# The overflow rows of the next pair are gathered under the branch of the overflow's second product

## The chip, the cores and the metric

The kernel runs on one core of a Trainium2 chip. The metric is the time on the device in microseconds; times of several runs are given as their median with the lowest and highest. A profile is one more execution under the hardware profiler, with a time of its own.

## What is computed

One layer of a diffusion backbone with 256 latent and 256 context tokens of width 1024: four parallel token mixers (attention, neighbourhood attention, Fourier mixing, convolution), merged and projected, and then a mixture of 16 experts, each token going to two of them. The change concerns the experts alone:

```python
out = jnp.zeros_like(t)
for e in range(N_EXPERTS):
    a, b = jnp.split(t @ w_gu[e], 2, axis=-1)
    out = out + gate[:, e:e + 1] * ((jax.nn.silu(a) * b) @ w_down[e])
```

`gate[:, e]` is zero for a token that isn't routed to expert `e`, so the kernel computes only the rows of the tokens routed there. How many these are is known only when the program runs: 32 per expert on average (256 tokens, two of 16 experts each).

## The kernel before, in words

The token mixers and the routing come first; the experts start some 430 us into the span. Experts are taken in 8 pairs (`for pair in range(NPAIR)`, line 1154). Each expert has slots for its rows in blocks of 32. The first block of both experts of a pair is always computed. The second (rows 33 to 64) stands under `tc.If(both)` (lines 1167 and 1202), the third and fourth (rows 65 to 128, 64 rows at once, "the overflow") under two nested branches: the outer asks whether either expert of the pair overflows (line 1126, a bit of the register `fpair`), the inner whether this expert does (line 1128, a bit of `fmore`). Rows beyond 128 have a part of their own behind all pairs (line 1212).

The branches run on TensorE, VectorE and ScalarE, each with its own copy of the flags. On the way past a branch an engine's sequencer computes the bit and compares it (two instructions); where the body is skipped it goes to a false block, which waits until the engine's own earlier work is done and raises its semaphore by what the body would have added, and then joins the rest.

The overflow of one expert has three parts:

- `more_gather(e)` (line 960): a one-hot matrix of the rows from the routing keys (VectorE, `ohv`), 8 matmuls that gather the rows (`gav`), two copies to SBUF (`rw`, one on ScalarE and one on VectorE), the gate values (`gsv`), 8 transposes (`gtv`) and 8 modulations in turn on VectorE and ScalarE (`hgv`).
- `more_up(e, hg)` (line 988): the first product, 16 matmuls with w_gu (`guv`, in the records two for each), then silu and the product with the other half (`siv`).
- `more_down(e, gsl, si)` (line 999): the transposed hidden rows (`htv`, `hTv`), their places (`otv`, `oTv`), the second product with w_down (`yv`), the gate (`ysv`), the split in two parts (`yhv`, `ylv`), and the scatter by matmuls onto the tokens (`scv`), which VectorE adds to `xs`.

A pair runs in this order on TensorE: the first product of the first blocks (`gu`), under `both` that of the second blocks, the overflow's first product, the gates (`gs`), the scatter of the pair before (`sce`, from its `Y`), the hidden rows transposed (`ht`), the places of the rows (`ote`, from the keys that POOL copies into `kr`), in pairs 1, 3 and 5 the gather of the next two pairs (`gag`), the overflow rows of the next pair, the second product (`y`, begun with a product by zeros that clears a bank), under `both` that of the second blocks, the overflow's second product with its scatter. Then `gated` (line 892) takes `y` times gate on VectorE and splits it, and the next pair begins. For pair 0 the overflow rows are gathered directly ahead of its first product, under a branch of their own. The framework's scheduler moves some matmuls of a product behind the branches that follow it in the text: in the trace the last 12 records of `y` and `gu` stand behind them.

The weights come from HBM by SP's queue, 1 MB per transfer, 12 transfers per pair, into 18 slots in all; a transfer waits until TensorE has read what was in its slot. All DMAs of the change's surroundings are these; the change itself holds none.

Of the kernel before, what the change touches and what calls it, by code (L numbers as in the profile page):

```python
# [54 lines left out]
def mixer_moe(ctx: ExitStack, tc: tile.TileContext, A, out, dbg=None):  # L55
# [18 lines left out]
    def pt(tag, name):  # L74
        return banks["pool"].tile([P, 512], F32, tag=tag, bufs=banks["n"][tag], name=name)
# [4 lines left out]
    def sc_t(name):  # L80
        return pt("sc", name)

    def tr_t(name):
        return pt("tr", name)
# [651 lines left out]
    def scr_t(*shape):  # L736
        n = int(np.prod(shape))
        t = scratch[:, n_scratch[0] : n_scratch[0] + n]
        n_scratch[0] += n
        axes = "abc"[: len(shape)]  # L740
        return t.rearrange(f"p ({' '.join(axes)}) -> p {' '.join(axes)}", **dict(zip(axes[1:], shape[1:])))
# [17 lines left out]
    two = scr_t(N8, 2, 4)  # L759
# [51 lines left out]
    def mm(*a, **k):  # L811
        tc.keep_in_program_order(PE.matmul(*a, **k))  # L812

    def tr(*a):
        tc.keep_in_program_order(PE.transpose(*a))
# [29 lines left out]
    def modulated2(dst, src, k):  # L845
        if k % 2:
            SC.activation(dst, src, AF.Identity, scale=a2[:, k : k + 1], bias=sh2[:, k : k + 1])
        else:
            V.tensor_scalar(dst, src, a2[:, k : k + 1], sh2[:, k : k + 1], op0=ALU.mult, op1=ALU.add)
# [110 lines left out]
    def more_gather(e):  # L960

        oh = onehot(f"v{e}", lambda t: key[:, t, e : e + 1], CAP, "ohv", 1)
        rows = ep.tile([P, 2, 512], F32, name=f"rw{e}", tag="ys", bufs=1)
        for h in range(2):
            g = sc_t(f"gav{e}{h}")
            i = 0
            for t in range(NT):
                for src in (xh, xl):
                    mm(g[:CAP, :], oh[t], src[:, t, 512 * h : 512 * h + 512], start=(i == 0), stop=(i == 2 * NT - 1))
                    i += 1  # L970
            (V.tensor_copy if h else SC.copy)(rows[:CAP, h, :], g[:CAP, :])
        tp = tr_t(f"gsv{e}")
        for p in range(2):
            for t in range(NT):
                mm(tp[64 * p : 64 * p + 64, 0:2], oh[t].bitcast(F32), gate[:, t, e : e + 1].to_broadcast([P, 2]),
                   start=(t == 0), stop=(t == NT - 1))
        gsl = ep.tile([P, 1], F32, name=f"gslv{e}", tag="gslv", bufs=4)
        V.tensor_copy(gsl, tp[:, 0:1])
        hg = ep.tile([P, NK, CAP], F32, name=f"hgv{e}", tag="hgv", bufs=2)
        tp = tr_t(f"gtv{e}")  # L980
        for k in range(NK):
            d = tp[:, CAP * k : CAP * (k + 1)]
            tr(d, rows[:CAP, k // 4, P * (k % 4) : P * (k % 4 + 1)], ident[:CAP, :CAP])
        for k in range(NK):
            modulated2(hg[:, k, :], tp[:, CAP * k : CAP * (k + 1)], k)
        return hg, gsl

    def more_up(e, hg):
        acc = pt("y", f"guv{e}")
        for k in range(NK):  # L990
            wv = W[e][0][k].rearrange("p (a j n) -> p a j n", a=2, j=2)
            for p in range(2):
                mm(acc[64 * p : 64 * p + 64, :].rearrange("p (a n) -> p a n", a=2), hg[:, k, :], wv[:, :, p, :],
                   start=(k == 0), stop=(k == NK - 1))
        si = ep.tile([P, 256], F32, name=f"siv{e}", tag="siv", bufs=2)
        hidden(si, acc)
        return si

    def more_down(e, gsl, si):
        tp = tr_t(f"htv{e}")  # L1000
        turn_hidden(tp, si)
        hT = ep.tile([P, 2, 128], F32, name=f"hTv{e}", tag="hTv", bufs=1)
        V.tensor_copy(hT.rearrange("p c s -> p (c s)"), tp[:, :256])
        ohT = compared(places(f"v{e}", lambda t: key16[:, t, e : e + 1].to_broadcast([P, P])), 2, f"v{e}")
        y = pt("gu", f"yv{e}")
        for f in range(4):
            r = 64 * (f // 2)
            for p in range(2):
                mm(y[64 * p : 64 * p + 64, :], hT[:, f % 2, r : r + 64], W[e][1][f][:, 512 * p : 512 * p + 512],
                   start=(f == 0), stop=(f == 3))  # L1010
        ys = ep.tile([P, 2, 512], F32, name=f"ysv{e}", tag="ys", bufs=1)[:, 0, :]
        Y = [ep.tile([P, 512], F32R, name=f"y{n}v{e}", tag=f"y{n}v", bufs=1) for n in "hl"]
        for c in range(2):
            s = slice(256 * c, 256 * c + 256)
            V.scalar_tensor_tensor(ys[:, s], y[:, s], gsl, G2[0][:, s], op0=ALU.mult, op1=ALU.mult)
            split(Y[0][:, s], Y[1][:, s], ys[:, s])
        for t in range(NT):
            for j in range(2):
                r = slice(64 * j, 64 * j + 64)
                scatter(f"v{e}", t, j, [(ohT[r], v[r]) for v in Y])  # L1020
# [100 lines left out]
    NPAIR = NE // 2  # L1121
    rows_of, si_of = {}, {}

    def more_of(pair, f):

        with tc.If((fpair & (1 << (8 + pair))) > 0):  # L1126
            for e in (2 * pair, 2 * pair + 1):
                with tc.If((fmore & (1 << e)) > 0):
                    f(e)

    def scatter_pair(pair):
        for t in range(NT):
# [21 lines left out]
    for pair in range(NPAIR):  # L1154
        if 0 < pair < NPAIR - 1:
            load_units(12)

        blocks = [pt("gu", f"gu{pair}{b}") for b in range(2)]
        mm(blocks[1], zero16[:, 0:1].to_broadcast([P, P]), zero16[:, 0:1].to_broadcast([P, 512]), start=True, stop=True)
        beside = first_steps if pair == 0 else (lambda k: None)  # L1160
        up_steps(blocks[0], members(pair, 0), range(NK), beside)
        flags, gate, gate2 = bits["fg"]
        fpe, fpair, fmore = (bits[n] for n in ("fpe", "fpair", "fmore"))
        if pair == NPAIR - 2:
            frest = nc.values_load(flags[0:1, 2:3], engines=engs + [ET.SP], min_val=0, max_val=top)
        both = (fpe & (1 << pair)) > 0
        with tc.If(both):
            up_steps(blocks[1], members(pair, 1), range(NK))
        si = ep.tile([P, 2, 256], F32, name=f"si{pair}", tag="si", bufs=1)
        for b in range(2):  # L1170
            hidden(si[:, b, :], blocks[b])
        if pair == 0:
            more_of(0, lambda e: rows_of.__setitem__(e, more_gather(e)))
        more_of(pair, lambda e: si_of.__setitem__(e, more_up(e, rows_of[e][0])))

        gp_ = gate_pair(pair)
        if pair:
            scatter_pair(pair - 1)
        gate_rows(pair, *gp_)
        tp = tr_t(f"ht{pair}")  # L1180
        for b in range(2):
            turn_hidden(tp[:, 256 * b : 256 * b + 256], si[:, b, :])
        hT = ep.tile([P, 2, 2, 128], F32, name=f"hT{pair}", tag="hT", bufs=1)
        SC.copy(hT.rearrange("p b c s -> p (b c s)"), tp)
        kr = key_rows(pair)
        tp = places(f"e{pair}", lambda t: kr[:, t].rearrange("p q e s -> p (q e s)"))
        ohTs[pair] = [compared(tp, c, f"e{pair}{c}", "oT", 2) for c in range(2)]
        if pair % 2 and pair + 1 < NPAIR:
            new_group(pair // 2 + 1)
            for k in range(NK):  # L1190
                group_step(pair // 2 + 1, k)
        if pair + 1 < NPAIR:
            more_of(pair + 1, lambda e: rows_of.__setitem__(e, more_gather(e)))
        if pair == NPAIR - 2:
            fng = pk[:, _PK["convw"][0] : _PK["convw"][0] + D]
            nc.sync.dma_start(fng, A["fng"].unsqueeze(0).to_broadcast([P, D]))

        ys_ = [pt("y", f"y{pair}{b}") for b in range(2)]
        mm(ys_[1], zero16[:, 0:1].to_broadcast([P, P]), zero16[:, 0:1].to_broadcast([P, 512]), start=True, stop=True)
        dns = [W[2 * pair + e][1] for e in range(2)]  # L1200
        down(ys_[0], hT[:, 0], dns, 0)
        with tc.If(both):
            down(ys_[1], hT[:, 1], dns, 1)
        more_of(pair, lambda e: more_down(e, rows_of[e][1], si_of[e]))
        Ys[pair] = [ep.tile([P, 2, 512], F32R, name=f"y{n}{pair}", tag=f"y{n}", bufs=1) for n in "hl"]
        ys = ep.tile([P, 2, 512], F32, name=f"ys{pair}", tag="ys", bufs=1)
        for b in range(2):
            gated(ys[:, b, :], ys_[b], gates_[pair][:, b : b + 1], b, *Ys[pair])
# [115 lines left out]
```

## Time and profile before

| what | value |
|---|---|
| median of 3 runs | 716.81 us |
| lowest, highest | 714.42, 717.22 us |
| profiled execution | 722.76 us, its span 721.0 us |
| TensorE busy (matmuls) | 640.1 us, 89% |
| VectorE busy | 412.8 us, 57% |
| ScalarE busy | 265.7 us, 37% |
| POOL busy | 71.9 us, 10% |
| mean granted clock of TensorE | 0.954 |
| DMA, mean over the span | 250 GB/s |

Times in the rows are microseconds from the start of the span, unless marked ns. PE is TensorE (matmuls), PEld its weight loads, DVE VectorE, ACT ScalarE, POOL GpSimd, SP SyncE; a q behind the name is the engine's sequencer, which runs branches and waits. L1126 is line 1126 of the kernel. The profiled execution is one run under the profiler and lies above the plain ones; durations come from it.

### The profile page before, as it was taken

Reading aid. Unit: us, or ns where it says so; the run is one execution under the profiler, and the core shown is the slowest. Engines: PE = TensorE matmul, PEld = TensorE weight load, DVE = VectorE, ACT = ScalarE, POOL = GpSimd, SP = SyncE. Lnnn points to the kernel's source line nnn. Section 1 sums busy time; section 2 is a strip of 40 time slices with the busy share of each in tenths; the row PEclk is TensorE's granted clock in tenths of the full one; section 3 lists DMA queues with packets and bytes.
Section 4 is the critical chain, followed back from the end, with each engine's and each line's share of the span. In section 5 each row is a group of like instructions: output and inputs, shape, how many; then the busy total and the mean of one; then the engine's idle time right before and its main releaser. Section 6 shows DMA issues by size and latency. Waiting matters only on the chain. (4 is left out here: it accounts for less than half of the span.)

```text
span 721.0 us, 12019 instructions
## 1 busy us (share of the span) xinstructions
PE 640.1 (89%) x4721; PEld 443.8 (62%) x4725; DVE 412.8 (57%) x806; ACT 265.7 (37%) x486; POOL 71.9 (10%) x112
## 2 busy tenths in 40 slices
PE   3769899999999998999999967889889979998992
PEld 0269899987887898989899952343324224333230
DVE  0179889988888787585766553351343243303334
ACT  2066947367755533343445441230012111300112
POOL 0123300021302000313111010000000000000001
PEclk9969999999999999999999988899989999999895
DMA  9794582533543696768698560999997999998001
GB/s 362 277 340 130 177 286 64 170 119 118 170 136 99 247 314 210 252 224 264 219 370 287 175 234 4 397 408 407 408 409 285 409 406 409 407 385 347 1 2 62
DMA packets 75121, 180.07 MB, mean 250 GB/s; under 512 B 3104, under 2 KB 39072, under 8 KB 74016
## 3 DMA queue, kind: packets, MB, share of 16 engines
q1 hardware_dynamic: 73232, 173.42, 66.0%
q0 software_dynamic: 1104, 3.15, 1.4%
q10 hardware_dynamic: 704, 2.42, 0.8%
q8 instruction: 52, 0.85, 0.5%
q14 instruction: 29, 0.24, 0.1%
HBM read 177.92 MB, written 1.05 MB: 248 GB/s over the span
## 5 line engine op out<-in xcount | busy, mean ns | idle before, releaser
L812 PE MATMUL gu<-we,hg 128*32 128x512 f32 x832 | 101.5, 606 | 3.7 <-PEq L1126 2.4
L290 PE MATMUL gl<-hhil,wl_gl 128*128 128x256 f32 x256 | 72.9, 287 | 1.8 <-DVE wl_gl L278 1.7
L290 PE MATMUL gl<-hhil,wh_gl 128*128 128x256 f32 x256 | 73.3, 287 | 0.0
L290 PE MATMUL gl<-hlol,wh_gl 128*128 128x256 f32 x256 | 72.3, 283 | 0.0
L812 PEld LDWEIGHTS gu<-we,hg 128*32 128x32 f32 x832 | 28.3, 111 | 68.5 <-issue 59.3
L812 PE MATMUL y<-we,hT 128*32 128x512 f32 x416 | 59.8, 649 | 6.1 <-PEq L1126 5.6
L277 ACT CAST wh_gl<-w_gl 128x1024 fp32r<-128x1024 f32 x32 | 33.1, 1049 | 50.0 <-PE gl L290 25.4
L458 DVE SCALAR_TENSOR_TENSOR cv<-zp,pk,cv 128x256 f32<-128x256 f32 x120 | 51.2, 478 | 0.2
L290 PEld LDWEIGHTS gl<-hhil,wl_gl 128*128 128x128 f32 x256 | 48.0, 188 | 3.9 <-DVE wl_gl L278 3.3
L290 PEld LDWEIGHTS gl<-hhil,wh_gl 128*128 128x128 f32 x256 | 48.1, 188 | 1.5 <-issue 1.5
L290 PEld LDWEIGHTS gl<-hlol,wh_gl 128*128 128x128 f32 x256 | 48.3, 189 | 0.5 <-issue 0.5
L290 PE MATMUL z<-y,wh_br 128*128 128x256 f32 x256 | 47.6, 283 | 0.0
L278 DVE TENSOR_TENSOR wl_gl<-w_gl,wh_gl 128x1024 fp32r<-128x1024 f32 x32 | 41.0, 1294 | 9.8 <-ACT wh_gl L277 9.6
L194 DVE SCALAR_TENSOR_TENSOR acc<-wv,csil,acc 128x512 f32<-128x512 f32 x56 | 40.3, 747 | 7.8 <-DMA wv<-in_w_mod_dram 7.8
L812 PEld LDWEIGHTS y<-we,hT 128*32 128x32 f32 x416 | 14.9, 115 | 42.2 <-issue 39.9
L290 PEld LDWEIGHTS z<-y,wh_br 128*128 128x128 f32 x256 | 39.6, 188 | 0.9 <-issue 0.7
L374 ACT CAST yh<-ys 64x512 fp32r<-64x512 f32 x32 | 19.7, 617 | 51.5 <-DVE ys L894 51.1
L290 PE MATMUL z<-y,wl_br 128*128 128x256 f32 x128 | 36.8, 289 | 1.5 <-DVE wl_br L278 1.5
L894 DVE SCALAR_TENSOR_TENSOR ys<-y,gsl,G 128x512 f32<-128x512 f32 x16 | 12.0, 750 | 37.5 <-PE y L812 17.3
L674 POOL TENSOR_TENSOR merged<-merged,gt 128x512 f32<-128x512 f32 x12 | 19.3, 1610 | 117.6 <-DVE gt L673 117.6
L876 DVE TENSOR_TENSOR si<-si,gu 128x256 f32<-128x256 f32 x16 | 6.6, 418 | 42.5 <-ACT si L875 42.5
L166 PE MATMUL mod<-wm,csil 128*32 128x512 f32 x64 | 15.2, 843 | 14.4 <-DVE csil L155 9.0
(411 smaller groups left out, 1514.0 us busy)
## 6 DMA issues: line engine op xcount, KB each, us to landing
we<-in_w_gu_dram SPq DMA_DIRECT2D x64, 1024.0 KB, 13.3
we<-in_w_down_dram SPq DMA_DIRECT2D x32, 1024.0 KB, 18.4
wv<-in_w_mod_dram SPq DMA_DIRECT2D x16, 1024.0 KB, 5.5
w_gl<-in_w_in_dram SPq DMA_DIRECT2D x16, 1024.0 KB, 5.7
wm<-in_w_mod_dram SPq DMA_DIRECT2D x8, 1024.0 KB, 9.4
w_br<-in_w_branch_dram SPq DMA_DIRECT2D x8, 1024.0 KB, 5.9
w_out<-in_w_out_dram SPq DMA_DIRECT2D x4, 1024.0 KB, 6.4
w_gq<-in_w_in_dram SPq DMA_DIRECT2D x2, 1024.0 KB, 8.1
```

What stands on the lines that cost most here:

```text
L166: PE.matmul(acc[32 * j : 32 * j + 32, :], csil[:, k, :], wm[:, 512 * j : 512 * (j + 1)], start=(k == 0), stop=(k == NK - 1))
L194: V.scalar_tensor_tensor(acc[:, s], wm[:, k % 2, s], csil[:, k, 0:1], acc[:, s], op0=ALU.mult, op1=ALU.add)
L277: SC.copy(w[0], raw[:, s])
L278: sub(w[1], raw[:, s], w[0].bitcast(F32), op=ALU.subtract)
L290: PE.matmul(dst, a, b, start=(k == 0 and wi + xi == 0), stop=(k == kt - 1 and wi == 1))
L374: SC.copy(hi, src)
L458: V.scalar_tensor_tensor(cv[:, ct, :], zp[:, ct, j : j + S], convw[:, ct, j : j + 1], cv[:, ct, :], op0=ALU.mult, op1=ALU.add)
L674: G.tensor_tensor(mt, mt, gts[c], op=ALU.add)
L812: tc.keep_in_program_order(PE.matmul(*a, **k))
L876: V.tensor_tensor(si, si, acc[:, n:], op=ALU.mult)
L894: V.scalar_tensor_tensor(ys, y, gsl, G2[flip], op0=ALU.mult, op1=ALU.mult)
```

## The change

`more_of(pair, f)` is replaced by helpers. The rows of the next pair are no longer gathered under an outer `If` of their own ahead of the second product; they are gathered behind the overflow's second product, in one joint outer `If` (`more_rest`) that is entered if this pair or the next one overflows. Within it, each of the two experts of this pair and each of the two of the next has its inner `If`, as before. For pair 0, rows and first product of an expert stand under one outer and one inner `If` (`more_first`). The bodies `more_gather`, `more_up` and `more_down` are unchanged.

```diff
-    def more_of(pair, f):
+    def if_more(bit, f):
+        with tc.If((fmore & (1 << bit)) > 0):
+            f(bit)
+
+    def of(pair):
+        return (2 * pair, 2 * pair + 1)
+
+    def rows_for(e):
+        rows_of[e] = more_gather(e)
+
+    def up_for(e):
+        si_of[e] = more_up(e, rows_of[e][0])
+
+    def more_first():
+        with tc.If((fpair & (1 << 8)) > 0):
+            for e in of(0):
+                if_more(e, lambda e: (rows_for(e), up_for(e)))
+
+    def more_ups(pair):
         with tc.If((fpair & (1 << (8 + pair))) > 0):
-            for e in (2 * pair, 2 * pair + 1):
-                with tc.If((fmore & (1 << e)) > 0):
-                    f(e)
+            for e in of(pair):
+                if_more(e, up_for)
+
+    def more_rest(pair):
+        two = pair + 1 < NPAIR
+        with tc.If((fpair & ((3 if two else 1) << (8 + pair))) > 0):
+            for e in of(pair):
+                if_more(e, lambda e: more_down(e, rows_of[e][1], si_of[e]))
+            if two:
+                for e in of(pair + 1):
+                    if_more(e, rows_for)
...
-        if pair == 0:
-            more_of(0, lambda e: rows_of.__setitem__(e, more_gather(e)))
-        more_of(pair, lambda e: si_of.__setitem__(e, more_up(e, rows_of[e][0])))
+        more_ups(pair) if pair else more_first()
...
-        if pair + 1 < NPAIR:
-            more_of(pair + 1, lambda e: rows_of.__setitem__(e, more_gather(e)))
...
-        more_of(pair, lambda e: more_down(e, rows_of[e][1], si_of[e]))
+        more_rest(pair)
```

## Rows read from the trace of the kernel before

**Rows 1.** Windows: us, busy us of each engine (instructions), granted clock, DMA share, GB/s.
```profile
480.00:524.00 44.00, 40.35 (x283) 14.44 (x286) 11.15 (x23) 5.71 (x12) 0.53 (x2) 1.00 1.03 408
583.00:590.00 7.00, 4.22 (x17) 0.74 (x13) 0.83 (x2) 1.23 (x2) 0.00 (x0) 0.76 1.03 404
```

**Rows 2.** Waits, 440 to 721 us: total us, times, longest (PE, then PEld).
```profile
PE y L812 <- PEq L1126: 6.0, 9, 2.8
PE gav L812 <- DVE ohv L840: 1.7, 2, 0.9
...
PEld gu L812 <- DMA we<-in_w_gu_dram: 1.3, 2, 1.0
```

**Rows 3.** Line 1126: engine, operation, count, ns min/median/max, first and last start.
```profile
L1126 PEldq ALU_OP  x24: 36/36/36, 446.5 to 697.7; - x24
L1126 PEldq COMPARE_BRANCH  x24: 67/220/2310, 446.7 to 697.8; - x24
...
L1126 PEldq EVENT_SEMAPHORE  x18: 51/51/51, 447.0 to 700.2; - x18
```

**Rows 4.** Line 1128, the inner branches, the same view.
```profile
L1128 PEldq ALU_OP  x12: 36/36/36, 475.2 to 660.3; - x12
...
L1128 PEldq EVENT_SEMAPHORE  x6: 51/51/51, 476.3 to 660.1; - x6
```

**Rows 5.** Timeline of TensorE: start, us, operation [idle before]; pairs 2, 3, 4, 7.
```profile
513.18 0.27 PE L812 MATMUL ote<-ident,kr 128*128 128x128 bf16 x2 [0.36 <-DVE gsl L950]
513.66 0.38 PE L812 MATMUL y<-zero 128*128 128x512 bf16 x1 [0.21 <-PEq L1126]
...
558.55 6.20 PE L812 MATMUL y<-we,hT 128*32 128x512 f32 x52 [0.46 <-PEq L1126]
...
580.65 0.38 PE L812 MATMUL y<-zero 128*128 128x512 bf16 x1 [0.43 <-ACTq L1126]
...
693.53 0.27 PE L812 MATMUL ote<-ident,kr 128*128 128x128 bf16 x2 [0.36 <-DVE gsl L950]
693.64 0.38 PE L812 MATMUL y<-zero 128*128 128x512 bf16 x1
```

**Rows 6.** Timeline of TensorE in pair 1: gather of the rows, `y`.
```profile
477.08 0.42 PE L812 MATMUL gav<-xh,ohv 128*64 128x512 f32 x1 [0.87 <-DVE ohv L840]
...
480.66 2.77 PE L812 MATMUL y<-we,hT 128*32 128x512 f32 x20 [0.25 <-issue]
484.32 1.91 PE L812 MATMUL y<-we,hT 128*32 128x512 f32 x12 [0.89 <-PEq L1126]
```

**Rows 7.** Timeline of TensorE in pair 5: the same places.
```profile
614.49 0.42 PE L812 MATMUL gav<-xh,ohv 128*64 128x512 f32 x1 [0.88 <-DVE ohv L840]
...
624.47 1.91 PE L812 MATMUL y<-we,hT 128*32 128x512 f32 x12 [0.19 <-PEq L1126]
```

**Rows 8.** Timeline of TensorE in pair 2: first product, end of `y`.
```profile
486.48 13.36 PE L812 MATMUL gu<-we,hg 128*32 128x512 f32 x116
500.41 7.09 PE L812 MATMUL guv<-we,hgv 128*64 128x512 f32 x32 [0.56 <-PEq L1128]
...
530.27 3.63 PE L812 MATMUL y<-we,hT 128*32 128x512 f32 x12
```

**Rows 9.** Timeline of TensorE: the longest gaps, in pairs 0 and 4.
```profile
449.57 0.56 PE L812 MATMUL gs<-gate,ohg 128*128 128x4 f32 x2 [3.27 <-PEq L1126]
...
586.50 3.37 PE L812 MATMUL y<-we,hT 128*32 128x512 f32 x12 [2.77 <-PEq L1126]
```

**Rows 10.** Line 1126 on TensorE from 446 to 450 us (pair 0).
```profile
L1126 PEldq ALU_OP  x2: 36/36/36, 446.5 to 447.1; - x2
L1126 PEldq COMPARE_BRANCH  x2: 230/1133/2036, 446.7 to 447.2; - x2
```

**Rows 11.** Line 1126 on TensorE from 583 to 587 us (pair 4).
```profile
L1126 PEldq COMPARE_BRANCH  x1: 2310/2310/2310, 584.0 to 584.0; - x1
```

**Rows 12.** DMA queues of the page: packets, MB, share of 16 engines.
```profile
q8 instruction: 52, 0.85, 0.5%
```

## Prediction

> **What bounds the kernel now.** I read the waits of TensorE over the stage of the experts first (440 us to the end), then the windows, then the timeline of TensorE pair by pair. The windows show TensorE busy 40.35 of 44 us in the stretch of pair 2, with the DMA engines full beside it [rows 1]. So two resources are near their limit, and the question is which one is waited for. The waits answer it: the largest single item is TensorE behind its own sequencer at line 1126, the outer `If` of the overflow (6.0 us in 9 waits), and the weights cost only 1.3 us on the side of the weight loads, in two waits that lie beside running matmuls [rows 2]. From about 456 us on, one long chain of TensorE sets the end; the DMA runs full because slots come free at TensorE's pace. A microsecond put on or taken off TensorE's order between two pairs therefore moves the end by about a microsecond.
>
> **What the branches do.** The view of line 1126 has 24 evaluations on TensorE, of which 18 pass through the false block (its semaphore instruction); line 1128 has 12 inner evaluations and 6 false ones [rows 3, 4]. Two inner evaluations each for rows, first and second product make 12, so only two pairs overflow; by their place these are pair 2 and pair 6, one expert each. Here is the count for the changed kernel. Outer `If`s: two in each of 8 pairs, 16 in place of 24. Entered are the first product's in pairs 2 and 6 and the new joint one in pairs 1, 2, 5 and 6 (own pair or next), so 10 are skipped. Inner ones: 2 in each of the two first products, 4 in each of the four joint branches, 20 in place of 12, of which 4 + 2 = 6 are entered (each rows, first and second product once per overflowing expert) and 14 skipped. **Evaluations: 36 before, 36 after; skipped: 24 before, 24 after.** The change saves no evaluation in this run of data. It moves them out of pairs without overflow into the pairs around one. What counts is the price at the old and at the new place.
>
> **Removed.** (a) The rows' `If` of the next pair, between the turn of the keys and the zero product of `y`, skipped in pairs 0, 2, 3, 4, 6. Where no `If` stands (pair 7), the zero product starts 0.11 us after `ote` does; in pair 2 it is 0.48, so 0.37 each. Pair 4 shows 0.43 idle where pair 2 shows 0.21, so 0.58; pair 3 has 0.46 idle [rows 5]. Pair 6 repeats pair 2, pair 0 is taken like it. Sum 3 x 0.37 + 0.46 + 0.58 = 2.15 us. (b) In pairs 1 and 5 the gaps around the gather: 0.87 and 0.88 before it, 0.25 behind it each, and the skipped second product's `If`, 0.89 and 0.19: 3.3 us [rows 6, 7]. Together 5.5 us.
>
> **Added.** A skip chained behind another one is not hidden. Its price has three rows: two evaluations follow each other at 446.5 and 447.1 (0.6) [rows 10]; the gap after two skips is 0.89 and after one 0.19, so 0.70 [rows 6, 7]; entering and skipping one inner `If` costs 0.56, 0.37 above the 0.19 [rows 8]. I take 0.53, between them, with 0.37 and 0.70 as ends. Pair 1: 0.89 as now for skipping the pair's second half and coming to the next evaluation, then three inner skips (own two experts, one of the next pair), 0.89 + 1.59 = 2.48, and 0.25 behind the gather: 2.7. Pair 5: 0.56 with one skip, two more, 0.25: 1.9. Pairs 2 and 6: the two experts of the next pair are evaluated behind the scatter of the own overflow, 2 x 0.53 = 1.06 each, 2.1. Together 6.7 us, with the ends 5.3 and 8.2. **Net: +1.2 us, from -0.2 to +2.7.**
>
> **The gather itself.** Its matmuls run in either place at the same price. Its one-hot rows, for which TensorE now waits 1.7 us in two waits [rows 2], are made under the first part of `y` after the change, so this part of the old gap has no successor. Behind the gather, VectorE's and ScalarE's steps for it now stand ahead of `gated`, whose products are read by the scatter of the next pair, behind the whole first product (13.36 us in pair 2 [rows 8]): covered; without that cover some 3 us per gather. `y` of pairs 1 and 5 comes 3.6 us earlier (480.66 less 477.08 [rows 6]), so w_down's slots and SP's loads come earlier by as much; the DMA is full there and TensorE doesn't wait for it: nothing. VectorE, ScalarE: as many evaluations as before, off the path. POOL has no part in these branches.
>
> **Pair zero.** Two outer `If`s become one. But the second took a branch of 2.04 us, with 3.27 us idle in all [rows 9, 10], four times any ordinary one. In this pair the two skips lie directly behind each other, and the long one is at the end. If what it waits for is the code at the far end, one skip over both bodies waits for the same code until the same moment. I take 0; the bound for a gain is the short branch's turn, 0.6, or all of the 2.04.
>
> **Clock.** [...] The new gap of pair 1 (2.5 us in one piece, where 0.87 and 0.89 lay apart) is nearest to pair 4's. I add 1.46 once; the ends are 0 and twice that, for pair 5.
>
> **The sum.** 1.2 + 1.46 = +2.7 us. On the profiled execution (722.76 us, its span 721.0) that is 725.5. That execution stands 6 us above the median of the plain runs, so the forecast goes by the median: 716.81 + 2.7 = **719.5 us**.
>
> [...] The long branches (2.04 and 2.31 us among 24 with a median of 0.22 [rows 3, 10, 11]) wait for something that the others don't. The trace also has a queue of 52 instruction transfers, 0.85 MB [rows 12]. The joint `If` is skipped over two more bodies than the old one (28 matmuls per second product, 24 per gather, by the code), so it jumps nearly twice as far in pairs 0, 3 and 4. [...]
>
> **Rivals.** (1) Slower: a longer skip meets a further long wait. Price by pair 4: 2.77 - 0.19 idle and 1.46 of slow matmuls, 4.0 us. One more: 723.5; two: 727.5. For it: two long ones already among short skips, and a jump twice as long in pairs 0, 3 and 4; against it: a wait seen under the profiler may be shorter without it. [...] (2) Faster: the code between the branches shrinks and shifts, pair 4's wait is gone and nothing takes its place: 719.5 - 4.0 = 715.5, and with the low price of a skip and no slow clock in pair 1, 716.8 - 0.2 - 4.0 = 712.6. (3) No loss of clock: 718.0, the range of no change.
>
> **How the numbers follow.** The forecast's own case has 0.45 and reaches from 716.6 (-0.2) to 722.4 (+2.7 and 2.9 of clock); (3) has 0.10, (1) 0.30, (2) 0.15. A measurement tells about 0.5%, 3.6 us. Within it lie three quarters of the forecast's case, (3) and the weak half of (2) without its low ends: 0.47. Slower: (1) and the upper quarter of the forecast's: 0.40. Faster: 0.13. The range for 8 in 10 reaches into (1) up to one long wait over the upper clock price, and into (2) to its middle: 714 to 726.
>
> **What would show it.** The view of line 1126 should count 16 evaluations in place of 24, the inner line 20 in place of 12, with 24 false blocks in all: otherwise the count is wrong. Right: `y`'s zero product starts 0.1 us after `ote` in every pair; in pairs 1 and 5 the gather stands behind `y` with 1.7 to 2.5 us idle ahead of it; one more stretch at the lower clock near 480 us. Rival 1: three or more branches over 1 us. Rival 2: one or none. What would make it wrong above all: a long wait that comes or goes with the place of the code.

## Result and profile after

| | before | after |
|---|---|---|
| median, lowest to highest (9 runs each) | 715.47, 714.42 to 719.35 us | 722.07, 720.03 to 723.31 us |
| ratio after to before, 95% interval | | 1.0078 [1.0058, 1.0098] |
| profiled execution, its span | 722.76, 721.0 us | 720.03, 718.2 us |
| mean granted clock of the profiled span | 0.954 | 0.967 |

The change makes the kernel slower by 0.6 to 1.0%. The forecast of 719.5 us was 2.6 us too low; the range (714 to 726) holds the time. As a difference to before, 2.7 us were forecast and 5.6 came (0.78% of 715.5). The two profiled executions mislead here: that of before lies above all of its 9 plain runs, that of after is the fastest of its 9. Set side by side they would say that the change gains 2.7 us. So both kernels were profiled once more, and the comparisons below use before's second profile (span 713.4 us, clock 0.967, as in the first profile of after).

The branch lines of after on TensorE (1139 is pair zero's outer `If`, 1144 that of the first product, 1151 the joint one, 1125 the inner one; columns as in [rows 3]):

```profile
L1139 PEldq COMPARE_BRANCH  x1: 2312/2312/2312, 443.3 to 443.3; - x1
L1139 PEldq EVENT_SEMAPHORE  x1: 51/51/51, 445.6 to 445.6; - x1
...
L1144 PEldq COMPARE_BRANCH  x7: 68/215/1147, 462.1 to 682.0; - x7
L1144 PEldq EVENT_SEMAPHORE  x5: 51/51/51, 462.6 to 684.5; - x5
...
L1151 PEldq COMPARE_BRANCH  x8: 68/202/347, 449.2 to 694.8; - x8
L1151 PEldq EVENT_SEMAPHORE  x4: 51/51/51, 450.9 to 697.3; - x4
...
L1125 PEldq ALU_OP  x20: 36/36/36, 476.4 to 666.7; - x20
L1125 PEldq EVENT_SEMAPHORE  x14: 51/51/51, 476.7 to 667.1; - x14
```

1 + 7 + 8 = 16 outer and 20 inner evaluations, and 1 + 5 + 4 + 14 = 24 false blocks: the count of the prediction, beside 24, 12 and 24 before [rows 3, 4].

Waits of TensorE in the stage of the experts of after (430 to 719 us; us in total, times, longest), which answer to [rows 2]:

```profile
PE gav L812 <- DVE ohv L840: 4.3, 2, 2.4
PE gu L812 <- PEq L1144: 3.1, 5, 1.7
PE gs L812 <- PEq L1139: 2.9, 1, 2.9
...
PE gu L812 <- issue: 2.4, 1, 2.4
PE y L812 <- PEq L1125: 2.0, 2, 1.0
...
PE y L812 <- PEq L1151: 1.2, 3, 0.8
```

And its timeline of TensorE at the places of [rows 6 to 9] (pairs 1, 2, 4, 5, 6; start, us, operation, idle before):

```profile
473.15 2.77 PE L812 MATMUL y<-we,hT 128*32 128x512 f32 x20 [0.16 <-issue]
478.35 0.41 PE L812 MATMUL gav<-xh,ohv 128*64 128x512 f32 x1 [2.43 <-DVE ohv L840]
...
481.61 1.91 PE L812 MATMUL y<-we,hT 128*32 128x512 f32 x12
...
527.45 3.48 PE L812 MATMUL y<-we,hT 128*32 128x512 f32 x12 [0.95 <-PEq L1125]
...
571.38 1.91 PE L812 MATMUL gu<-we,hg 128*32 128x512 f32 x12 [1.68 <-PEq L1144]
...
581.14 1.91 PE L812 MATMUL y<-we,hT 128*32 128x512 f32 x12 [0.81 <-PEq L1151]
...
583.30 1.05 PE L812 MATMUL gu<-we,hg 128*32 128x512 f32 x2
586.71 5.80 PE L812 MATMUL gu<-we,hg 128*32 128x512 f32 x52 [2.36 <-issue]
...
618.37 0.41 PE L812 MATMUL gav<-xh,ohv 128*64 128x512 f32 x1 [1.83 <-DVE ohv L840]
...
667.51 3.59 PE L812 MATMUL y<-we,hT 128*32 128x512 f32 x12 [1.02 <-PEq L1125]
```

The reader is to see three things. `y` of pairs 1 and 5 now comes first, and the gather stands behind it with 2.43 and 1.83 us idle. Pairs 2 and 6 have a new gap of about 1 us behind the overflow. And in pair 4 the 2.77 us of [rows 9] are gone from `y` (0.81), but the first product has 1.68 us ahead of its last part, and that of pair 5 stands 2.36 us after two records, with no branch at the place.

Where the time went, stage by stage, from one start of `ote` to the next (the last from pair 7's to the end), in the second profile of before and the first of after. The last column is the prediction's own sum for the stage (removed and added together, without the clock):

| from `ote` of pair | before, us | after, us | difference | predicted |
|---|---|---|---|---|
| 0 (starts 447.25, 447.85) | 21.67 | 20.70 | -0.97 | -0.37 |
| 1 (468.92, 468.55) | 41.10 | 41.64 | +0.54 | +0.72 |
| 2 (510.02, 510.19) | 39.50 | 40.15 | +0.65 | +0.69 |
| 3 (549.52, 550.34) | 26.27 | 26.80 | +0.53 | -0.46 |
| 4 (575.79, 577.14) | 27.89 | 28.63 | +0.74 | -0.58 |
| 5 (603.68, 605.77) | 43.84 | 44.42 | +0.58 | +0.58 |
| 6 (647.52, 650.19) | 39.23 | 40.36 | +1.13 | +0.69 |
| 7 (686.75, 690.55) to the end | 26.65 | 27.65 | +1.00 | 0 |
| sum | | | +4.2 | +1.3 |

The predicted values of stages 1 and 5 are the added 2.73 and 1.9 less the removed 2.01 and 1.32 of [rows 6, 7]. One caution: before's own two profiles differ by up to 1.4 us in a stage (the first has 20.23, 40.50, 29.25 and 40.48 us in stages 0, 2, 4 and 6), and by their clock. A difference of less than that in the table counts only where a row of the timeline bears it out.

### The profile page after: what moved, and what is told of

Its sections match the earlier page's. It is cut to its first block, busy times and chain, and to the rows that moved or that the text cites. A ratio compares the mean times of both kernels' runs of the same rounds, so it can differ in the third digit from the quotient of the medians.

```text
span 718.2 us, 12029 instructions
## 1 busy us (share of the span) xinstructions
PE 634.4 (88%) x4720; PEld 440.7 (61%) x4725; DVE 415.0 (58%) x806; ACT 265.7 (37%) x486; POOL 71.8 (10%) x112
## 3 DMA queue, kind: packets, MB, share of 16 engines
HBM read 177.92 MB, written 1.05 MB: 249 GB/s over the span
## 5 line engine op out<-in xcount | busy, mean ns | idle before, releaser
L875 ACT ACTIVATE si<-gu 128x256 f32<-128x256 f32 x16 | 6.0, 382 | 61.6 <-PE gu L812 50.4
```

Source lines behind the costliest of these rows:

```text
L875: SC.activation(si, acc[:, :n], AF.Silu)
```

## Experiments

Theory A: the long waits are for code, and a change of the program's layout moves them. Theory C: merging pair zero's branches costs. Theory D: the new nest behind the second product costs, by chained skips or by the gather's place. Theory E came up on the way: a skip in the middle of a product costs a further round of matmuls.

**1. Before, once more.** No edit.

> The kernel before, unchanged, for a second profiled execution. Theory A (the time between the kernels is in TensorE's waits for its next code, which hang on where in the program a skipped branch lands): the long branches of the before profile stand in every execution of this program, so the 2036 ns branch of pair zero and the 2310 ns branch of pair four are found again at the same two places, and the ratio is 1.000. Rival B (those two waits are chance, of one execution): at least one of the two is gone or has moved, and the span falls by the 2.8 us that its gap showed, towards the plain median of 715.5.

Ratio 0.9995 [0.9966, 1.0024]. Its profile: the two long gaps in the timeline (and the one of pair four's first product), the branch of pair four (line 1126, 579 to 581 us), and the DMA queue of instruction transfers from 579.5 to 582.5 us:

```profile
445.29 0.56 PE L812 MATMUL gs<-gate,ohg 128*128 128x4 f32 x2 [3.32 <-PEq L1126]
...
570.03 1.91 PE L812 MATMUL gu<-we,hg 128*32 128x512 f32 x12 [0.89 <-PEq L1126]
...
582.44 1.91 PE L812 MATMUL y<-we,hT 128*32 128x512 f32 x12 [2.88 <-PEq L1126]
```
```profile
L1126 PEldq COMPARE_BRANCH  x1: 2410/2410/2410, 579.9 to 579.9; - x1
```
```profile
q8 instruction: 1, 0.02, 2.5%
```

Both waits are at the two places of [rows 9 to 11]; they belong to the program, not to the execution. The 7.6 us by which this span is shorter than the first profile's are 3.8 us ahead of the experts (the first `cum` starts at 425.04 instead of 428.81 us, in code that is the same) and, behind it, mostly the clock (its mean is 0.967 here and 0.954 there): the same 12 records of `y` behind the wait took 3.37 us [rows 9] and here 1.91.

**2. Pair zero alone.**

```diff
-        if pair == 0:
-            more_of(0, lambda e: rows_of.__setitem__(e, more_gather(e)))
-        more_of(pair, lambda e: si_of.__setitem__(e, more_up(e, rows_of[e][0])))
+        def first(e):
+            if pair == 0:
+                rows_of[e] = more_gather(e)
+            si_of[e] = more_up(e, rows_of[e][0])
+        more_of(pair, first)
```

> Before, with only the rows and the first product of pair zero under one branch; the next pairs' rows stay at their old place. One outer evaluation fewer in all (23 outer, 12 inner). Theory A: pair zero keeps one long branch of about 2.3 us, and all later code moves up by a few instructions, so pair four's long branch can stay or vanish: 716 if it stays, about 713 if it goes. Rival C (the pair zero part costs the 6.6 us by itself): about 722. Rival D (the cost is the nest behind the second product): 715.5, as before.

Ratio 0.9988 [0.9959, 1.0016]; one long branch (2088 ns) stays in pair zero. Theory C falls.

**3. The rest alone.** The change, with pair zero as before.

```diff
-        more_ups(pair) if pair else more_first()
+        if pair == 0:
+            with tc.If((fpair & (1 << 8)) > 0):
+                for e in of(0):
+                    if_more(e, rows_for)
+        more_ups(pair)
```

> The changed kernel, with the rows of pair zero back under an outer branch of their own. 17 outer and 20 inner evaluations. Theory D (the chained inner skips beside pairs two and six, and the gather's place, cost the time): 722, as the full change. Rival C (pair zero): 715.5 to 717. Theory A: between 716 and 724, decided by how many branches of over 1 us its profile has; the full change has two (2312 and 1147 ns) and one wait with no branch of 2.4 us in pair five.

Ratio 1.0056 [1.0025, 1.0088]. Most of the loss, within the noise all of it, is in the part behind the second product.

**4. The place without the nest.**

```diff
-        if pair + 1 < NPAIR:
-            more_of(pair + 1, lambda e: rows_of.__setitem__(e, more_gather(e)))
 ...
         more_of(pair, lambda e: more_down(e, rows_of[e][1], si_of[e]))
+        if pair + 1 < NPAIR:
+            more_of(pair + 1, lambda e: rows_of.__setitem__(e, more_gather(e)))
```

> Before, with the next pair's rows moved behind the overflow's second product, but each under an outer branch of its own: the new place without the new nest (24 outer, 12 inner evaluations, as before). Theory D as the nest (chained inner skips at .52 us each beside the two overflowing pairs): the nest's share is gone, so 715.5 to 717. Theory D as the place (the gather's work for pairs two and six now starts later): about 722. Theory A: 716 to 724 by the number of branches of over 1 us in its profile, 2.3 to 3 us for each that before does not have.

Ratio 1.0092 [1.0065, 1.0118], no better than the nest, so the nest can't be the whole loss. Its timeline in pairs 0, 2 and 4:

```profile
447.68 1.89 PE L812 MATMUL y<-we,hT 128*32 128x512 f32 x2 [0.30 <-PEq L1200]
450.24 5.35 PE L812 MATMUL y<-we,hT 128*32 128x512 f32 x30 [0.68 <-PEq L1126]
...
527.48 5.28 PE L812 MATMUL y<-we,hT 128*32 128x512 f32 x12
...
586.12 2.87 PE L812 MATMUL y<-we,hT 128*32 128x512 f32 x10 [2.04 <-PEq L1126]
```

Two records of `y`, one matmul, stand alone between two branches in pair 0 and take 1.89 us (as one matmul does in pair 0 of after, at a granted clock of 0.50; in pairs 1 and 4 here it is 1.02 us); the last 12 records of pair 2 take 5.28 us where before needs 3.63 [rows 8]. The program's order explains it. `y` of a pair is 16 matmuls, which go to four groups of 32 columns in turn, and four at a time run beside each other (8 records, four matmuls, of `gu` take 1.06 us at 439.50 us of before's second profile, one matmul alone 1.02). In before the scheduler issues 10 of them (in pairs 1 to 7), then the branches, then 6; here 10, then a branch, 1, a second branch, 5. A skipped branch waits in its false block until TensorE's own earlier work is done: in pair 0 of after the joint branch is through by 449.6 us, and its semaphore instruction comes at 450.9, with the end of the one matmul that runs from 449.00 to 450.89. So each piece would pay for a last, unfilled round. That is theory E; experiments 8 to 11 test it.

**5. The same work, other code places.** 11 matmuls more in the skipped first product of expert 2, 20 in that of expert 8; none runs. The two numbers were chosen by counting TensorE's instructions in the program, to move the place in the code at which pair four's skip lands.

```diff
         acc = pt("y", f"guv{e}")
+        for _ in range({2: 11, 8: 20}.get(e, 0)):
+            wv = W[e][0][0].rearrange("p (a j n) -> p a j n", a=2, j=2)
+            mm(acc[0:64, :].rearrange("p (a n) -> p a n", a=2), hg[:, 0, :], wv[:, :, 0, :], start=True, stop=True)
```

> Before, with 11 more matmuls in the skipped first product of expert 2 and 20 in that of expert 8 (each repeats the first matmul of the product; none of them runs on this data). Nothing that is executed changes; only the place of later code moves, by 44 and by 124 TensorE instructions. Theory A (long waits are for code, and their place depends on where a skip lands): pair four's branch of 2.3 to 2.4 us is gone from the profile, its gap ahead of the last matmuls of y falls from 2.8 to 0.9 us, and the time falls by 2 to 4 us: ratio 0.995 to 0.997. Rival (the long wait belongs to the length of that skip or to the traffic at that moment): the branch stays over 2 us, ratio 1.000.

Ratio 0.9962 [0.9940, 0.9983]. Its outer branch in pair four (line 1129 there), and the timeline:

```profile
L1129 PEldq COMPARE_BRANCH  x1: 215/215/215, 579.8 to 579.8; - x1
```
```profile
569.13 1.06 PE L812 MATMUL gu<-we,hg 128*32 128x512 f32 x7 [0.69 <-PEq L1129]
571.09 1.05 PE L812 MATMUL gu<-we,hg 128*32 128x512 f32 x5 [0.90 <-issue]
...
580.23 1.91 PE L812 MATMUL y<-we,hT 128*32 128x512 f32 x12 [0.68 <-PEq L1129]
```

2410 ns became 215, and the gap 0.68; a smaller wait without a branch (0.90) appeared in the first product. Code that never runs moves this kernel by 0.4%. So the place of the code decides over pair four's wait, and the rival, which kept it over 2 us, falls. That TensorE waits there for a transfer of its code was not shown: it is the author's reading, from one such transfer beside the wait in experiment 1 (0.02 MB in 579.5 to 582.5 us). These waits are lumps (1.49 to 3.32 us in experiments 1, 6, 7 and 12) that a change of this size can move, though it need not: experiment 2 left both where they were (2.79 us in pair zero, 2.73 in pair four).

**6. The change without its chained skips.** The rows of pairs 3 and 7 go under their own first product. Not shown in the diff: two matmuls that don't run, in the first product of expert 6, hold the later code nearly in its place.

```diff
...
-                if_more(e, up_for)
+                if_more(e, (lambda e: (rows_for(e), up_for(e))) if pair in (3, 7) else up_for)
...
-        two = pair + 1 < NPAIR
+        two = pair + 1 < NPAIR and pair not in (2, 6)
```

> The changed kernel, but the rows of pairs three and seven are gathered under the branch of their own first product (as pair zero's), so that the two inner evaluations chained behind the overflow in pairs two and six are gone (16 inner in place of 20). 2 matmuls that don't run keep the later code within 2 instructions of its place. Theory of the prediction (a chained evaluation costs 0.53 us beside the overflow): the 1.06 us in pair two and about as much in pair six come off, 2.1 us: ratio to before 1.004 to 1.005 where the full change has 1.008. Rival (the chain is covered, the time went to code waits): 1.007 to 1.008.

Ratio 1.0039 [1.0021, 1.0056], at the edge of what was expected and clear of the rival's 1.007. The long waits of the change are still there (3.20, 1.49 and 2.33 us against its 2.94, 1.68 and 2.36), so the gain isn't theirs. Timeline, end of `y` in pairs 2 and 6, now without the gaps of 0.95 and 1.02 us:

```profile
528.64 3.63 PE L812 MATMUL y<-we,hT 128*32 128x512 f32 x12
...
669.25 3.44 PE L812 MATMUL y<-we,hT 128*32 128x512 f32 x12
```

**7. The change with both suspects undone.** In addition to what 6 changes, the rows of pairs 2 and 6 are gathered ahead of `y` again (the diff is against the change; the two matmuls of 6 that don't run are left out).

```diff
...
-                if_more(e, up_for)
+                if_more(e, (lambda e: (rows_for(e), up_for(e))) if pair in (3, 7) else up_for)
...
-        two = pair + 1 < NPAIR
+        two = pair + 1 < NPAIR and pair not in (1, 2, 5, 6)
...
+        if pair in (1, 5):
+            with tc.If((fpair & (1 << (9 + pair))) > 0):
+                for e in of(pair + 1):
+                    if_more(e, rows_for)
         ys_ = [pt("y", f"y{pair}{b}") for b in range(2)]
```

> The change with both suspected places undone: the rows of pairs two and six are gathered ahead of y as before (own outer branch in pairs one and five), those of pairs three and seven under their own first product (no chained evaluation); the joint branch stays in pairs zero, three and four. The theory that the exposed gather in pairs one and five (a wait of 2.4 and 1.8 us for its one-hot rows, and lower clock behind it) and the chains make the cost: ratio 0.998 to 1.002, and the gaps ahead of gav are back at 0.9 us. Rival (the cost is in the code waits of pair four): 1.004, as without the chains alone.

Ratio 1.0004 [0.9980, 1.0027]. The gather's gaps are back at their size of [rows 6, 7], while the change's wait in pair five is still there:

```profile
474.91 0.41 PE L812 MATMUL gav<-xh,ohv 128*64 128x512 f32 x1 [0.87 <-DVE ohv L840]
...
585.14 7.43 PE L812 MATMUL gu<-we,hg 128*32 128x512 f32 x49 [2.29 <-issue]
...
610.71 0.42 PE L812 MATMUL gav<-xh,ohv 128*64 128x512 f32 x1 [0.88 <-DVE ohv L840]
```

The long waits are again those of the change (2.89, 1.60 and 2.29 us). So of 0.78% the chains make about 0.4 and the gather behind `y` about 0.35, each a difference of two ratios and known to some 0.3 either way. What is left of the change, with all five rows' `If`s of the prediction's removed term (a) gone, takes as long as before. By the table it is the long waits of pairs four and five that eat what the saved branches give.

**8 to 11. Branches behind the whole product.** The conditions of TensorE are computed behind the last matmul that stands ahead of them in the text; such a product is called pinned here. Experiment 8 pins both products of before, 9 both of the change, 10 both of experiment 4, and 11 the second product of before alone:

```diff
+    def behind(cond, body):
+        cur = nc.cur_bb
+        n = len(cur.bb.instructions)
+        last = next(x for x in reversed(cur.bb.instructions) if x.engine == ET.PE)
+        with tc.If(cond()):
+            body()
+        for x in cur.bb.instructions[n:]:
+            if x.engine == ET.PE and type(x).__name__ == "InstRegisterAlu":
+                tc.add_manual_dep(x, last.name, mybir.DependencyInfo(mybir.DependencyClass.NoSync, mybir.DependencyReason.DATA),
+                                  reason="behind")
+                break
...
-        with tc.If(both):
-            down(ys_[1], hT[:, 1], dns, 1)
+        behind(lambda: (fpe & (1 << pair)) > 0, lambda: down(ys_[1], hT[:, 1], dns, 1))
```

> Before, with TensorE's branch conditions (both and overflow, of either product) computed behind the last matmul of the product that stands ahead of them in the text. In the kernel before, the scheduler leaves the last 6 of the 16 or 32 matmuls of each product behind the branches. Four matmuls on the four column groups run at once (6 take 1.91 us, 10 take 2.77 us, so about 0.93 us for a round of up to four). Theory E (a skip in the middle of a product drains TensorE and costs a round of its own): 3 + 2 rounds become 4, 0.9 us less at each of 16 places, up to 14 us: 702 to 710. Rival (the last six matmuls stood there because their weights come late, or the DMA, full in these stretches, is the bound): 714 to 717, with waits for DMA in place of the drained rounds. Slower rival: the skips' 0.2 to 0.9 us, now at the end of a product, meet the waits of the next steps: 718 to 720.

> The changed kernel with the same order: each branch condition of TensorE behind the last matmul of its product. Theory E: 16 rounds of 0.9 us fewer, 708 to 716; the difference to the pinned kernel before stays the 4 to 5 us of the change, if that comes from chained skips and the exposed gather, and falls if it comes from the broken products of the joint branch. Rival: 720 to 723, as the change.

> The rows behind the second product under an outer branch of their own (which took 1.009 of before), now with TensorE's conditions computed behind the last matmul of each product. Theory E (that kernel lost by breaking y in three parts, 10, 1 and 5 matmuls, 3 + 1 + 2 rounds where before has 3 + 2): it gains more from the order than the kernel before did (0.6%), 1.3 to 1.8%: ratio 0.992 to 0.997. Rival (it lost by the place of the gather, whatever the order of y): gain 0.6%, ratio 1.003.

> Before, with only the conditions behind the second product pinned, those behind the first product left to the scheduler. With both pinned the ratio was 0.994, with new waits of 0.6 to 1.5 us for weights of the first product. If the pin of y makes the gain (8 rounds of 0.93 us, less the weights' limit): 0.989 to 0.993. If that of gu makes it: 0.997 to 1.000.

| kernel | as the scheduler has it | behind the products |
|---|---|---|
| before, both products | 1 | 0.9937 [0.9915, 0.9958] |
| before, second product alone | 1 | **0.9918 [0.9889, 0.9948]** |
| the change, both products | 1.0078 | 1.0042 [1.0017, 1.0068] |
| experiment 4, both products | 1.0092 | 0.9971 [0.9950, 0.9993] |

The groups of `y` (line, engine, form, count; busy us, mean ns; idle before) in the second profile of before, then in the kernel with the second product pinned:

```profile
L812 PE MATMUL y<-we,hT 128*32 128x512 f32 x416 | 58.8, 647 | 5.3 <-PEq L1126 5.2 <-DMA we<-in_w_gu_dram 0.2
```
```profile
L812 PE MATMUL y<-we,hT 128*32 128x512 f32 x416 | 47.6, 608 | 0.0
```

And its timeline in pair 1 and pair 4:

```profile
475.47 3.64 PE L812 MATMUL y<-we,hT 128*32 128x512 f32 x32
480.01 0.38 PE L812 MATMUL gu<-zero 128*128 128x512 bf16 x1 [0.90 <-PEq L1125]
...
486.92 3.63 PE L812 MATMUL gu<-we,hg 128*32 128x512 f32 x30 [0.65 <-DMA we<-in_w_gu_dram]
...
578.48 0.38 PE L812 MATMUL gu<-zero 128*128 128x512 bf16 x1 [1.97 <-PEq L1125]
```

All 32 records in one piece take 3.64 us; in two pieces they take 2.77 + 1.91 = 4.68 [rows 6]. 1.04 us in each of the seven pairs whose `y` is split is 7.3; the measured gain is 5.9 us (0.82% of 716.8). The rows show where a part goes again: the gap moves to the start of the next product, and weights are waited for there. So theory E holds for the second product (experiment 11 came as expected), and experiment 4 gains more than before does (1.2% against 0.6), a little less than the 1.3 to 1.8 expected.

Its sizes for both products were misses. Before was expected at 702 to 710 us and took 711.76, and both products pinned gain no more than the second alone; in the profile the first product waits 1.51 and 1.18 us for weights, such waits as the rival had named. The change was expected at 708 to 716 and took 720.21, its distance to the pinned kernel before 1.05%, 7.5 us, where 4 to 5 were expected to stay. Its profile has a new wait without a branch, in the first product of pair 1:

```profile
458.43 1.83 PE L812 MATMUL gu<-we,hg 128*32 128x512 f32 x12 [3.72 <-issue]
```

The split of `y` is not what the change lost by, since the change keeps the 10 and 6 of before in all pairs but zero. The kernel before with the second product in one piece has the lowest ratio of all here; its interval overlaps that of both products pinned.

**12. The change, once more.** No edit.

> The changed kernel, unchanged, once more. Its first profiled execution was the fastest of nine (720.03 beside a median of 722.07) and shows no stretch at the lower clock behind the 2.4 us gap of pair one; the execution without the chains, with the same gap, shows one of 6.8 us at 478 us. If the clock behind that gap is what separates the plain runs from the first profile: a stretch near 478 or near 587 us in this profile, or, where the profile has none, a time near 720 again. If the place of code decides alone: the same three long waits as in the first profile (ahead of gs 2.9, of gu 1.7 and of gu 2.4 us) at the same places. The ratio: 1.005 to 1.009.

Ratio 1.0072 [1.0042, 1.0101], as expected; the profiled execution took 724.18 us, its span 722.4. Timeline in pair 1, and the granted clock there (in the row of a window, the third number from the right):

```profile
479.59 0.45 PE L812 MATMUL gav<-xh,ohv 128*64 128x512 f32 x1 [2.46 <-DVE ohv L840]
...
481.34 0.63 PE L812 MATMUL gav<-xh,ohv 128*64 128x512 f32 x1
...
483.90 3.63 PE L812 MATMUL y<-we,hT 128*32 128x512 f32 x12
```
```profile
480.00:488.00 8.00, 8.00 (x41) 3.13 (x43) 3.27 (x8) 2.63 (x6) 0.00 (x0) 0.57 1.03 408
```

The three long waits stand at the places of the first profile (2.84, 1.49 and 2.33 us; 2.94, 1.68 and 2.36 there). New is the clock: behind the gap of pair 1 it is 0.57 of full over these 8 us (in the first profile 1.00, from 473 to 487 us), a gather matmul goes from 0.39 to 0.63 us and `y`'s last part from 1.91 to 3.63. From `ote` of pair 1 (469.81) to that of pair 2 (514.20) this execution takes 44.39 us, the first profile 41.64: 2.75 us. Five executions with a gap of 2.4 to 2.6 us at this place were profiled (the change twice, experiments 3, 6 and 9); three of them show the fall (this one, 6 and 9; in 9 the gap is 2.62 us, and the gather's matmuls behind it take 0.63 us each).

## Why the prediction was right or wrong

- **The count** was right: 36 evaluations and 24 skips on both sides, moved, not saved.
- **What is removed** was right in kind. `y`'s zero product starts 0.11 us behind `ote` in pairs 2, 4 and 6 (510.19 to 510.30, 577.14 to 577.25), as it did in pair 7 alone [rows 5]. "In every pair" could not come: in pairs 1, 3 and 5 the gather of the next two pairs stands between, and pair 3 gave back 0.26 us (from `ote` to `y` 4.60 in place of 4.86) where 0.46 was forecast.
- **The gather behind `y`** was right in size (2.43 and 1.83 us against 2.48 and 1.62), in part by luck. The text said that the one-hot rows would be made under `y`, so that their part of the old gap would have no successor. VectorE's row says otherwise:

```profile
477.85 0.36 DVE L840 SCALAR_TENSOR_TENSOR ohv<-pk,key 128x64 fp32r<-128x64 f32 x2 [4.75 <-PEq L1125]
```

  VectorE was idle for 4.75 us. It was through its own branches by 474.2 us and stood on until TensorE's false blocks had raised the semaphore (the last at 477.8), so the rows were not made early. Of the 2.43 us, TensorE's skips took 1.93 (475.92 to 477.85), less than the 2.48 forecast for them, and the one-hot rows the other 0.50, forecast at nothing. The two errors cancel.
- **The chains** in pairs 2 and 6 were right: 1.06 us each against gaps of 0.95 and 1.02, and experiment 6 shows that taking them out gives 2.8 us (the difference of 1.0078 and 1.0039, known to about 1.9 us either way).
- **Pair zero** at 0 was right (experiment 2). That its stage gained 0.97 instead of 0.37 says little: against before's first profile (20.23 us) it lost 0.47. `y` starts 1.15 us behind `ote` where before has 2.15, but it is broken into 1 and 15 matmuls, and the granted clock, 0.50 behind the long gap in after, is back at 1.00 by 453 us there; in before's second profile the product by zeros takes 0.58 us at 447.82 and 0.39 again at 455.68.
- **The clock** was right in kind and half right in size. 1.46 us once was the forecast, the 3.37 us of [rows 9] less the 1.91 of [rows 6], beside a granted clock of 0.76 over 583 to 590 us [rows 1]. That pair 1's gap would bring as much was an estimate, and no run shows that figure: a fall cost 2.75 us here, and it comes in some executions and not in others. The price itself was of that kind: pair four's gap brought a fall in before's first profile [rows 9] and none in its second, with 2.88 us idle. The first profile of after has none in pair 1; the median of the plain runs lies 2 us above it.
- **The step that failed**, though the range held, is pair four: "a long wait that comes or goes with the place of the code" was named as what would make the forecast wrong, but the sum itself left the wait in place at no change. Rivals 1 and 2 took it as one wait more or one fewer. What came was both: the 2.88 us at `y` went (0.81), and 1.68 us in pair four's first product (0.89 before) and 2.36 in pair five's came. 3.77 us of gaps became 4.85. The wait in pair five's first product also breaks that product: it takes 18.57 us (583.30 to 601.87) in place of 15.18 (584.60 to 599.78), 3.39 more, of which 2.36 is the wait and about 1.0 a further round. The table has it: stages 3 and 4 were to gain 1.04 us and lost 1.27. That is 2.3 of the 2.9 us by which the stages miss. Experiment 7 says the same by medians: of the prediction's terms it keeps only the removed 2.15 us, which is a ratio of 0.997, and it measured 1.0004 [0.9980, 1.0027].
- **The last stage**, at 0 in the sum, shows +1.0 us, and 0.9 of it is the clock of that execution (granted 0.50 from 702 to 706 us). The last scatter's matmuls, ahead of the end:

```profile
700.71 0.40 PE L812 MATMUL sce<-yl,oTe 128*128 128x512 f32 x1
...
705.17 0.63 PE L812 MATMUL sce<-yl,oTe 128*128 128x512 f32 x1
```

  The first row is of before's second profile, the second of after: from `ote` to their ends it is 14.36 and 15.25 us. Before's first profile has the 0.63 too, so it is not peculiar to the change.
- **The test of rival 1**, three or more branches over 1 us, gave two (2312 and 1147 ns), and still it was half true: the third wait has no branch at all. It comes two records into a product, shortly after the landing of the longer joint skip, with one transfer of the instruction queue in those 3 us. Experiment 5 moved a wait by the place of the code alone (2410 ns became 215). That such a wait is for a fetch of code is the author's reading, which no run shows, for the waits without a branch at their place least of all.
- **The chances** leaned to no change (0.47) where the measured 0.6 to 1.0% is slower (0.40). The net of +1.2 was too near to zero by the 2.3 us above, and rival 1, with one more long wait at 723.5, came nearest. That the range held is owed to the room that it left for such waits, not to the sum.

What stays open: how much of the 0.35% of experiment 7 is the gather's gap and how much the clock behind it, which were undone together; and what exactly TensorE waits for in the waits without a branch.

## What to carry to other kernels

A branch that is skipped is not free where it stands in a stream: here it drained the engine (0.89 us idle ahead of `y`'s last part [rows 6], and 1.04 us for the split), so price it at its new place, count the pieces into which it cuts a product, and put it behind the last matmul of one. Merging branches of several bodies saves evaluations only where all of them are skipped; where one is entered, every other body under the same nest is asked for in turn, at about half a microsecond each here (0.95 and 1.02 us for two in pairs 2 and 6). Before a fraction of a percent is put down to an edit, profile both kernels twice and move their code by some instructions that never run: if the time follows by as much, the edit need not be the cause.

## What the hardware showed that was not expected

- A long wait of TensorE with no branch at its place (what it is for, no run shows): 2.36 us ahead of the third record of a product, 2.33 in the second profile of the change, 2.33 and 2.29 in experiments 6 and 7.
- The lower clock behind a gap of the same length is not certain: three of five executions; 2.75 us in the one where it was priced.
- 16 matmuls of 32 columns take 3.64 us in one piece and 4.68 in two; a single one alone takes about as long (1.02 us in experiment 4; 1.89 at a granted clock of 0.50 in pair 0 of after) as four beside each other (1.06 in before's second profile).
